# Three chunk buffers, a later gate product, smaller background steps and f16 selection in a two-block transformer kernel

## The chip, the cores and the metric

One core of one Trainium2 chip runs the whole program in one launch. The metric is the device time of one execution in microseconds (us). Engines are named as in the profile: PE (matmul), PEld (its weight loads), DVE (vector), ACT (scalar, which also issues DMAs), POOL (GpSimd, which issues the indirect DMAs), SP (which issues most DMAs).

## The reference, cut to what matters

Two blocks follow each other. The first has two layers; in each, a mixer (attention, pooling, a short convolution) is followed by a mixture of single experts. Layer 0 does this for 256 tokens and 256 context rows together, layer 1 for the 256 tokens. The experts are what the change is about:

```python
s1, i1 = lax.top_k(s[:, :, 0], 16)
s2, i2 = lax.top_k(s[:, :, 1], 16)
cand = (s1[..., :, None] + s2[..., None, :]).reshape(128, 8, 256)
cidx = (i1[..., :, None] * 128 + i2[..., None, :]).reshape(128, 8, 256)
top_s, pos = lax.top_k(cand, 16)
eidx = jnp.take_along_axis(cidx, pos, axis=-1)
gate = jax.nn.softmax(top_s, axis=-1)
hid = jax.nn.gelu(jnp.einsum('td,thkd->thk', xc, u_emb[eidx]))
return jnp.einsum('thk,thkd->td', gate * hid, v_emb[eidx])
```

Each row of 1024 values picks 8 times 16 of 16384 experts. An expert's number is 128 times a first index plus a second one, both below 128. The second block (feed-forward, retention, block attention, convolution) is not touched.

## The kernel before, in words

Every f32 matrix is multiplied as three products of halves: ACT rounds a 128 x 1024 weight tile `raw` to `wh` (`_high`, line 212), DVE or POOL subtracts to get the rest `wl` (`_low`, line 223), and PE multiplies high by high, high by low and low by high. `Stream` hands the tiles out in one fixed order (`plan`); its loads (`raw`, five buffers) are issued on SP as buffers come free. `pool_every = n` sends every n-th subtraction to POOL.

**The experts, dense part.** For three of layer 0's four tiles of 128 rows (384 columns, `TD`), and all of layer 1's, the kernel multiplies by all experts. In the *first expert stage* (loop over 128 tiles of `in_u`) PE computes x times u, ACT applies the gelu into `gstage` (line 1642) and stores two of them at a time to DRAM (`gel`, line 1647). Meanwhile the gates are worked out in the background and stored as a dense matrix (`gmat`, 128 experts by 32 rows at a time). In the *second expert stage* (loop over 128 tiles of `in_vv`) hidden values and gates come back in chunks: `wload` (lines 1595 and 1597, on SP) loads `gelc` and `gmc`, four steps' worth for layer 0 (`CI` = 4) and 768 KB each, `wmul` (line 1604, on DVE for layer 0) multiplies them in place, `wsplit` makes `Wh` (ACT, line 472) and `Wl` (DVE, line 473) for the step two ahead, and `vmm` (line 1692) does 18 matmuls of 512 columns a step. Two chunks have buffers: chunk c + 2 is loaded in the last step of chunk c, and chunk c + 1 multiplied in the first step of chunk c.

**The experts, gathered part.** Layer 0's fourth tile fetches the 128 rows of u and 128 rows of v that each of its rows needs by indirect DMAs (POOL, line 1399, four buffers of 128 x 1024), and DVE does one pass over each (line 1408 for u, 1423 for v). These 256 passes are spread: some in the first expert stage, some in the second, and the rest in the convolution part of layer 1's mixer (`tail`), where each of 35 units does its share. The modulation of layer 1 is made in the same second stage by DVE from tiles `in_modt` (line 516).

**The background.** In layer 0 `Side` decides where background pieces stand in the program: it counts a virtual time (`tick`, one step per few matmuls), books DVE and ACT time per piece (`took`, `use`), and lets a piece run when both engines' booked time lies at most `LIM` = 2000 ns ahead. A `yield step()` is a place where a weight tile's subtraction can come between two pieces. The pieces of `route`, for each tile of 128 rows: eight sums `cand` (line 1435), eight rounds of top 16, then for index and half a comparison `eq` (line 1463), its product with the index table `sif` (line 1465) and a sum (line 1466); then the gates, and from line 1556 the dense gate matrix.

```python
nc.vector.tensor_mul(eq, eq, sif[:, hh, i, None, :].to_broadcast([128, 4, 16, 16]))
```

In all of this the order on each engine is fixed when the program is built, and each engine runs its instructions in that order.

Of the kernel before, what the change touches and what calls it, by code (L numbers as in the profile page):

```python
# [10 lines left out]
F32 = mybir.dt.float32  # L11
# [249 lines left out]
LIM = 2000  # L261
# [8 lines left out]
class Side:  # L270
# [8 lines left out]
    def __init__(self, period, ring):  # L279
        self.lanes, self.lates = [], []  # L280
        self.period, self.ring = period, ring
        self.now = self.due = 0.0
        self.slot = [0.0] * 4
        self.free = {"a": 0.0, "v": 0.0, "p": 0.0}
        self.seq = 0
        self.floor = False
        self.rate, self.pe = RATE, 1.0

    def _advance(self, lane):
        try:  # L290
# [83 lines left out]
    def tick(self, dt):  # L374
        self.now += dt * self.pe
        while True:
            while any(x[0] <= self.now for x in self.lates):
                self._late()
            if self.now < self.due or max(self.free["v"], self.free["a"]) > self.now + LIM:
                return  # L380
            for lane in self.lanes:
                if self._ready(lane[1]) <= self.now:
                    self._run(lane)
                    break
            else:
                return
# [18 lines left out]
def tile_dit_peer_conformer(ctx: ExitStack, tc: tile.TileContext, A, out):  # L405
# [834 lines left out]
    def seg_tail(pool, ns, upd, halves, hs, ss, ab, banks, fill=None, then=None):  # L1240


        xs = two_rows(pool, upd, halves, hs[0:2], ss[0], 2 if fill is None else 4)

        def rest(*ts):
            for t in ts:
                for dh in halves:
                    upd(t, dh)

        if fill is None:  # L1250
            norm_cols(pool, xs, ab[0], 0, 2 if ns == 2 else 3, banks, then)
            W.pool_every = 0 if ns == 1 else 2
            W.pump(3)
            if ns == 2:
                rest(2)
            return
        rest(2)
        norm_cols(pool, xs, ab[0], 0, 3, banks, then)
        rest(3)
        xs = norm_rows(pool, hs[2:4], ss[1], 4)  # L1260
        for k in range(2):
            fill(k, 0)
        norm_cols(pool, xs, ab[1], 256)
        for k in range(2):
            fill(k, 1)
# [4 lines left out]
    def peer(l, hcp, kp, keys, early):  # L1270
# [14 lines left out]
        with ExitStack() as st:  # L1285
# [72 lines left out]
            TKW = 2.0  # L1358
            side = cur["side"] = W.side = Side(0.0 if sp else 24 * T / 2.4 / (nt + 1.3), ring)
            if sp:  # L1360
                side.rate, side.pe = RATE2, 1.09
            sel = select()
            side.add(sel)
            W.pool_every = 1
# [63 lines left out]
            def route():  # L1428
                for t in (range(nt) if not sp else (3, 0, 1, 2)):
                    v4 = sv[:, t].rearrange("p (h i) k -> p h i k", i=2)  # L1430
                    cand = tk.tile([128, 8, 16, 16], F32, name="cand", bufs=1)
                    if sp:
                        yield step()
                    for h in range(8):
                        (nc.vector if sp else nc.gpsimd).tensor_add(cand[:, h], v4[:, h, 0, :, None].to_broadcast([128, 16, 16]),
                                                                    v4[:, h, 1, None, :].to_broadcast([128, 16, 16]))
                    took("v", 3000)
                    ts = tk.tile([128, 8, 16], F32, name="ts", bufs=2)
                    pos = tk.tile([128, 8, 16], U32, name="pos", bufs=2)
                    yield step()  # L1440
# [11 lines left out]
                    nc.vector.tensor_scalar(ab[:, 1], pos, 15, None, op0=OP.bitwise_and)  # L1452
                    abf = tk.tile([128, 2, 8, 16], F32, name="abf", bufs=1 if sp else 2)
                    nc.vector.tensor_copy(abf, ab)
                    sif = tk.tile([128, 8, 2, 16], F32, name="sif", bufs=1 if sp else 2)
                    nc.vector.tensor_copy(sif, si[:, t].rearrange("p (h i) k -> p h i k", i=2))
                    took("v", 1100)
                    yield step()
                    for i in range(2):
                        for h0 in (0, 4):  # L1460
                            hh = slice(h0, h0 + 4)
                            eq = tk.tile([128, 4, 16, 16], F32, name="eq", bufs=1)
                            nc.vector.tensor_tensor(eq, abf[:, i, hh, :, None].to_broadcast([128, 4, 16, 16]),
                                                    iota16[:, None, None, :].to_broadcast([128, 4, 16, 16]), op=OP.is_equal)
                            nc.vector.tensor_mul(eq, eq, sif[:, hh, i, None, :].to_broadcast([128, 4, 16, 16]))
                            nc.vector.tensor_reduce(IN[:, t, i].rearrange("p (h k) -> p h k", h=8)[:, hh], eq, axis=AX.X, op=OP.add)
                            took("v", 3700)
                            yield step(TKW * 1.3)
                    nc.vector.tensor_sub(GN[t].rearrange("p (h k) -> p h k", h=8), ts, ts[:, :, 0:1].to_broadcast([128, 8, 16]))
                    if sp:  # L1470
# [84 lines left out]
                for q in range(0, TD // 4, 2):  # L1555
                    if sp:
                        yield paced(q)
                    Am = tg.tile([128, 8, 128], F16, name="Am", bufs=3)
                    Bk = tg.tile(shape, F16, name="Bk", bufs=2)
                    Bm = tg.tile([128, 2] + shape[1:], F16, name="Bm", bufs=3)  # L1560
                    nc.vector.tensor_tensor(Am, iotac[:, None, :].to_broadcast([128, 8, 128]),
                                            IT[:, 1, q * 4:q * 4 + 8, None].to_broadcast([128, 8, 128]), op=OP.is_equal)
                    nc.vector.tensor_tensor(Bk, iotas, spread(IT[:, 0], q), op=OP.is_equal)
                    took("v", 1950)
                    if len(pend) > 2:
                        flush(*pend.pop(0))
                    yield paced(q + 1)
                    for n in range(2):
                        nc.vector.tensor_mul(Bm[:, n], Bk, spread(GT[:, n], q))
                    done = took("v", 1420)  # L1570
                    if len(pend) > 2:
                        flush(*pend.pop(0))
                    pend.extend((q + j, Am[:, 4 * j:4 * j + 4], Bm[:, :, 2 * j:2 * j + 2], done) for j in range(2))
                    if not sp:
                        yield
# [15 lines left out]
            ld, ww = {}, {}  # L1591

            def wload(c):
                g = vq.tile([128, CI, TD], F32, name="gelc", bufs=2)
                nc.sync.dma_start(g, gel_d[c])
                m = vq.tile([128, ntb, CI, TB], F32, name="gmc", bufs=2)
                nc.sync.dma_start(m, g_d[:, :, c * CI:(c + 1) * CI, :].rearrange("b p c t -> p b c t"))
                ld[c] = (g, m)

# [11 lines left out]
            def wsplit(i):  # L1611
                c, r = divmod(i, CI)
                g = ld[c][0]
                wh = vp.tile([128, TD], F32R, name="Wh", bufs=4)
                wl = vp.tile([128, TD], F32R, name="Wl", bufs=4)
                split(wh, wl, g[:, r])
                if sp:
                    took("a", 470)
# [7 lines left out]
            for i in range(128):  # L1626
# [1 line left out]
                    wsplit(0)  # L1628
                    wsplit(1)
                if i % GB == 0:  # L1630
                    gs = gp.tile([128, GB, TD], F32, name="gstage", bufs=3)
                h, lo = W.next("u", l, i)
                half = i % per
                if half == 0:
# [17 lines left out]
                if i == 118:  # L1652
# [6 lines left out]
                    vp = st.enter_context(tc.tile_pool(name=f"pv{l}", bufs=2))  # L1659
                    vq_stack = ExitStack()  # L1660
                    vq = vq_stack.enter_context(tc.tile_pool(name=f"pw{l}", bufs=2))
                    wload(0)
                    wload(1)
                    if l == 0:
                        def turn():
                            for _ in angles(vq):
# [29 lines left out]

            for i in range(128):
                c, r = divmod(i, CI)
                if r == 0 and c + 1 < nch:
                    wmul(c + 1)  # L1700
                if i + 2 < 128:
                    wsplit(i + 2)
                if r == CI - 1 and c + 2 < nch:
                    wload(c + 2)
                hl = W.next("vv", l, i, 1 if i >= 126 else None)
                if i >= 126:
# [730 lines left out]
```

## Time and profile before

| what | us |
|---|---|
| median of 3 runs | 4544.48 (4543.31 to 4550.07) |
| the profiled execution's own time | 4539.79 |
| its span, first to last instruction | 4538.0 |
| PE busy | 4215.3 (93%) |
| DVE busy | 3221.3 (71%) |
| ACT busy | 1970.2 (43%) |
| POOL busy | 1128.6 (25%) |
| DMA moved | 932.29 MB, 205 GB/s over the span |

The profiled execution lies 4.7 us below the median of the runs. Busy PE is pipelined matmuls and not PE at its peak: the granted clock (1.00 is 2.4 GHz, 0.50 is 1.2 GHz) stands in the windows. Layer 0's first expert stage ends at about 1444 us, its second runs from there to about 2206 us, and the gathered rest ends at about 2372 us. Layer 1's second expert stage runs from 3144 to 3502 us.

### The profile page before, as it was taken

The page shows a single profiled execution, that of the slowest core. Times are in us where ns is not written, and L with a number is a line of the kernel's source. Part 1 is how long each engine was busy: PE and PEld are TensorE (multiplying, and loading weights), DVE is VectorE, ACT ScalarE, POOL GpSimd, SP SyncE. Part 2 cuts the span into 40 slices and gives each one's busy share as a digit, 9 for nine tenths or more (in the row PEclk, how much of TensorE's full clock was granted, in tenths as well). Part 3 has the DMA queues.
Part 4 walks back from the last instruction along what each step waited for, and adds up shares of the span by engine and source line. Part 5 has one row for each costly group of instructions (what it writes and reads, how often), then busy time and mean ns, then how long its engine had stood idle before and what let it go on. Part 6 is the DMA issues. An engine that isn't in the chain of part 4 may idle for free. (4 is left out here: it accounts for less than half of the span.)

```text
span 4538.0 us, 66430 instructions
## 1 busy us (share of the span) xinstructions
PE 4215.3 (93%) x25423; PEld 3735.4 (82%) x25423; DVE 3221.3 (71%) x5177; ACT 1970.2 (43%) x2939; POOL 1128.6 (25%) x871
## 2 busy tenths in 40 slices
PE   8999999999998877777779989999999999999999
PEld 5887878999997666666678879999887998999988
DVE  6747766999996766566786878786666577555855
ACT  4224443334662222222334444575445445444544
POOL 0012343333117412222543446201443000000000
PEclk9999999999999888888899989999999999999999
DMA  6532232456889877878783336778886644556344
GB/s 218 166 99 69 72 101 97 151 194 234 293 293 343 278 259 270 289 276 283 249 301 110 107 124 206 237 282 306 281 280 237 215 154 132 187 181 215 116 160 156
DMA packets 304824, 932.29 MB, mean 205 GB/s; under 512 B 27752, under 2 KB 95736, under 8 KB 299640
## 3 DMA queue, kind: packets, MB, share of 16 engines
q1 hardware_dynamic: 244000, 696.86, 46.1%
q0 software_dynamic: 37040, 135.29, 8.3%
q10 hardware_dynamic: 23464, 95.88, 5.6%
q8 instruction: 199, 3.26, 0.3%
q14 instruction: 121, 0.99, 0.1%
HBM read 841.94 MB, written 85.99 MB: 204 GB/s over the span
## 5 line engine op out<-in xcount | busy, mean ns | idle before, releaser
L212 ACT ACTIVATE wh<-raw 128x1024 fp32r<-128x1024 f32 (+1 forms) x1086 | 1131.4, 1045 | 1093.4 <-DMA raw<-in_vv 516.4
L469 PE MATMUL pA<-xH,wl 128*128 128x256 f32 (+2 forms) x4600 | 1422.0, 309 | 57.3 <-DVE wl L223 46.1
L223 DVE TENSOR_TENSOR wl<-raw,wh 128x1024 fp32r<-128x1024 f32 (+2 forms) x956 | 1185.5, 1249 | 365.2 <-issue 185.5
L467 PE MATMUL pA<-xH,wh 128*128 128x256 f32 (+2 forms) x4600 | 1439.6, 313 | 1.7 <-ACT xH L472 1.3
L468 PE MATMUL pA<-xL,wh 128*128 128x256 f32 (+2 forms) x4600 | 1417.2, 308 | 0.5 <-DVE xL L473 0.3
L469 PEld LDWEIGHTS pA<-xH,wl 128*128 128x128 f32 x4600 | 876.1, 190 | 93.0 <-DVE wl L223 55.4
L467 PEld LDWEIGHTS pA<-xH,wh 128*128 128x128 f32 x4600 | 877.0, 191 | 34.8 <-issue 6.0
L468 PEld LDWEIGHTS pA<-xL,wh 128*128 128x128 f32 x4600 | 877.1, 191 | 26.6 <-DVE xL L473 1.1
L223 POOL TENSOR_TENSOR wl<-raw,wh 128x1024 fp32r<-128x1024 f32 (+1 forms) x130 | 322.8, 2484 | 731.8 <-PE pA L469 362.8
L1692 PE MATMUL pA<-wl,Wh 128*128 128x512 f32 x1024 | 349.9, 424 | 150.4 <-DVE wl L223 150.4
L1692 PEld LDWEIGHTS pA<-wl,Wh 128*128 128x128 f32 x1024 | 203.2, 202 | 211.1 <-DVE wl L223 163.9
L1692 PE MATMUL pA<-wh,Wl 128*128 128x512 f32 x1024 | 344.5, 419 | 1.7 <-DVE Wl L473 1.7
L1692 PE MATMUL pA<-wh,Wh 128*128 128x512 f32 x1024 | 335.3, 409 | 6.2 <-ACT Wh L472 6.2
L1399 POOL DMA_INDIRECT gr<-in_ur,gi x128 | 185.8, 1451 | 530.9 <-DVE gr L1408 498.8
L468 PE MATMUL pA<-wl,xH 128*128 128x256 f32 (+2 forms) x800 | 272.1, 340 | 10.2 <-POOL wl L223 6.2
L467 PE MATMUL pA<-wh,xH 128*128 128x256 f32 (+2 forms) x800 | 277.9, 347 | 1.8 <-ACT xH L472 1.8
L469 PE MATMUL pA<-wh,xL 128*128 128x256 f32 (+2 forms) x800 | 271.5, 339 | 1.1 <-DVE xL L473 1.1
L1399 POOL DMA_INDIRECT gr<-in_vr,gi x128 | 176.3, 1377 | 340.1 <-DVE gx L1423 297.7
L1609 POOL TENSOR_TENSOR gelc<-gelc,gmc 128x256 f32<-128x256 f32 x128 | 147.9, 1189 | 422.4 <-DMA gmc<-gmat 398.6
L1692 PEld LDWEIGHTS pA<-wh,Wl 128*128 128x128 f32 x1024 | 206.8, 202 | 54.5 <-DVE Wl L473 2.4
L1692 PEld LDWEIGHTS pA<-wh,Wh 128*128 128x128 f32 x1024 | 200.3, 196 | 56.2 <-ACT Wh L472 6.5
L458 POOL TENSOR_TENSOR segr<-segr,nhalf 128x1 f32<-128x1 f32 (+1 forms) x24 | 13.9, 579 | 886.3 <-DVE segr L547 886.3
(456 smaller groups left out, 6305.4 us busy)
## 6 DMA issues: line engine op xcount, KB each, us to landing
raw<-in_u SPq DMA_DIRECT2D x256, 512.0 KB
raw<-in_vv SPq DMA_DIRECT2D x256, 512.0 KB
raw<-in_modt SPq DMA_DIRECT2D x80, 512.0 KB
gmat<-gst ACTq DMA_DIRECT2D x20, 2048.0 KB
raw<-in_conv SPq DMA_DIRECT2D x48, 512.0 KB
raw<-in_gate SPq DMA_DIRECT2D x48, 512.0 KB
gel<-gstage ACTq DMA_DIRECT2D x64, 384.0 KB
gelc<-gel SPq DMA_DIRECT2D x32, 768.0 KB
```

The source lines that it names most:

```text
L212: self.nc.scalar.activation(h[:, :w], t[:, :w], AF.Copy)
L223: e.tensor_sub(lo[:, :w], t[:, :w], h[:, :w].bitcast(F32))
L458: nc.gpsimd.tensor_tensor(r, r, nhalf[:, 0:1].to_broadcast([128, w]), op=OP.pow)
L467: nc.tensor.matmul(o, s[0], m[0], start=start, stop=False)
L468: nc.tensor.matmul(o, s[0], m[1], start=False, stop=False)
L469: nc.tensor.matmul(o, s[1], m[0], start=False, stop=stop)
L1399: nc.gpsimd.indirect_dma_start(t, None, tabs[j // 128], bass.IndirectOffsetOnAxis(ap=gi[:, k:k + 1], axis=0))
L1609: nc.gpsimd.tensor_mul(gv, gv, m[:, :, ci])
L1692: nc.tensor.matmul(acc[t][dh], s_, m_[:, dh * 512:(dh + 1) * 512], start=(i == 0 and n == 0), stop=(i == 127 and n == 2))
```

## The change

Layer 0 (`sp`) alone gets three buffers each for `gelc` and `gmc`: three chunks are loaded before its second expert stage, then chunk c + 3 in the third step of chunk c, and chunk c + 1 is multiplied in the third step of chunk c. In exchange `Wh` and `Wl` go from four buffers to three, and `gstage` from three to two. `Side` gets its own limit for DVE, 1200 ns in layer 0, and the steps of `route` are cut smaller. `eq` and `sif` become f16 in both layers. `pool_every` is 0 and no longer 2 after layer 0's experts.

```diff
@@ -286,3 +286,3 @@
         self.floor = False
-        self.rate, self.pe = RATE, 1.0
+        self.rate, self.pe, self.lim = RATE, 1.0, LIM
 
@@ -378,3 +378,3 @@
                 self._late()
-            if self.now < self.due or max(self.free["v"], self.free["a"]) > self.now + LIM:
+            if self.now < self.due or self.free["v"] > self.now + self.lim or self.free["a"] > self.now + LIM:
                 return
@@ -1251,3 +1251,3 @@
             norm_cols(pool, xs, ab[0], 0, 2 if ns == 2 else 3, banks, then)
-            W.pool_every = 0 if ns == 1 else 2
+            W.pool_every = 0
             W.pump(3)
@@ -1360,3 +1360,3 @@
             if sp:
-                side.rate, side.pe = RATE2, 1.09
+                side.rate, side.pe, side.lim = RATE2, 1.09, 1200
             sel = select()
@@ -1434,5 +1434,7 @@
                     for h in range(8):
+                        if sp and h == 4:
+                            yield step()
                         (nc.vector if sp else nc.gpsimd).tensor_add(cand[:, h], v4[:, h, 0, :, None].to_broadcast([128, 16, 16]),
                                                                     v4[:, h, 1, None, :].to_broadcast([128, 16, 16]))
-                    took("v", 3000)
+                        took("v", 380)
                     ts = tk.tile([128, 8, 16], F32, name="ts", bufs=2)
@@ -1454,3 +1456,3 @@
                     nc.vector.tensor_copy(abf, ab)
-                    sif = tk.tile([128, 8, 2, 16], F32, name="sif", bufs=1 if sp else 2)
+                    sif = tk.tile([128, 8, 2, 16], F16, name="sif", bufs=1 if sp else 2)
                     nc.vector.tensor_copy(sif, si[:, t].rearrange("p (h i) k -> p h i k", i=2))
@@ -1461,8 +1463,14 @@
                             hh = slice(h0, h0 + 4)
-                            eq = tk.tile([128, 4, 16, 16], F32, name="eq", bufs=1)
+                            eq = tk.tile([128, 4, 16, 16], F16, name="eq", bufs=1)
                             nc.vector.tensor_tensor(eq, abf[:, i, hh, :, None].to_broadcast([128, 4, 16, 16]),
                                                     iota16[:, None, None, :].to_broadcast([128, 4, 16, 16]), op=OP.is_equal)
+                            took("v", 1250)
+                            if sp:
+                                yield step()
                             nc.vector.tensor_mul(eq, eq, sif[:, hh, i, None, :].to_broadcast([128, 4, 16, 16]))
+                            took("v", 1250)
+                            if sp:
+                                yield step()
                             nc.vector.tensor_reduce(IN[:, t, i].rearrange("p (h k) -> p h k", h=8)[:, hh], eq, axis=AX.X, op=OP.add)
-                            took("v", 3700)
+                            took("v", 1250)
                             yield step(TKW * 1.3)
@@ -1562,4 +1570,5 @@
                                             IT[:, 1, q * 4:q * 4 + 8, None].to_broadcast([128, 8, 128]), op=OP.is_equal)
+                    took("v", 1250)
                     nc.vector.tensor_tensor(Bk, iotas, spread(IT[:, 0], q), op=OP.is_equal)
-                    took("v", 1950)
+                    took("v", 700)
                     if len(pend) > 2:
@@ -1593,5 +1602,5 @@
             def wload(c):
-                g = vq.tile([128, CI, TD], F32, name="gelc", bufs=2)
+                g = vq.tile([128, CI, TD], F32, name="gelc", bufs=3 if sp else 2)
                 nc.sync.dma_start(g, gel_d[c])
-                m = vq.tile([128, ntb, CI, TB], F32, name="gmc", bufs=2)
+                m = vq.tile([128, ntb, CI, TB], F32, name="gmc", bufs=3 if sp else 2)
                 nc.sync.dma_start(m, g_d[:, :, c * CI:(c + 1) * CI, :].rearrange("b p c t -> p b c t"))
@@ -1613,4 +1622,4 @@
                 g = ld[c][0]
-                wh = vp.tile([128, TD], F32R, name="Wh", bufs=4)
-                wl = vp.tile([128, TD], F32R, name="Wl", bufs=4)
+                wh = vp.tile([128, TD], F32R, name="Wh", bufs=3 if sp else 4)
+                wl = vp.tile([128, TD], F32R, name="Wl", bufs=3 if sp else 4)
                 split(wh, wl, g[:, r])
@@ -1630,3 +1639,3 @@
                 if i % GB == 0:
-                    gs = gp.tile([128, GB, TD], F32, name="gstage", bufs=3)
+                    gs = gp.tile([128, GB, TD], F32, name="gstage", bufs=2 if sp else 3)
                 h, lo = W.next("u", l, i)
@@ -1661,4 +1670,4 @@
                     vq = vq_stack.enter_context(tc.tile_pool(name=f"pw{l}", bufs=2))
-                    wload(0)
-                    wload(1)
+                    for c in range(3 if sp else 2):
+                        wload(c)
                     if l == 0:
@@ -1698,3 +1707,3 @@
                 c, r = divmod(i, CI)
-                if r == 0 and c + 1 < nch:
+                if r == (CI - 2 if sp else 0) and c + 1 < nch:
                     wmul(c + 1)
@@ -1702,3 +1711,5 @@
                     wsplit(i + 2)
-                if r == CI - 1 and c + 2 < nch:
+                if sp and r == CI - 2 and c + 3 < nch:
+                    wload(c + 3)
+                if not sp and r == CI - 1 and c + 2 < nch:
                     wload(c + 2)
```

Second expert stage of layer 0, SP's queue, the loads of two chunks among the weight tiles (`vv`) and modulation tiles (`modt`); before:

```order
L1595 DMA gelc<-gel_7_5865 128x1536
L1597 DMA gmc<-gmat_5890 128x12x128
L200 DMA raw<-in_vv 128x1024
L200 DMA raw<-in_modt 128x1024
L200 DMA raw<-in_vv 128x1024 x3
L1595 DMA gelc<-gel_8_5866 128x1536
```

and in the changed program:

```order
L1604 DMA gelc<-gel_8_5866 128x1536
L1606 DMA gmc<-gmat_5890 128x12x128
L200 DMA raw<-in_modt 128x1024
L200 DMA raw<-in_vv 128x1024 x2
L200 DMA raw<-in_modt 128x1024
L200 DMA raw<-in_vv 128x1024 x2
L1604 DMA gelc<-gel_9_5867 128x1536
```

The loads keep their distance of four weight tiles, but stand one chunk further ahead of their use. DVE in the same stage, from one gate product on; before (names with their numbers, which tell the chunks apart):

```order
L1604 TENSOR_TENSOR gelc_13922<-gelc_13922,gmc_13924 128x1536 [waits DMAHW7_49,DMAHW0_49]
L473 TENSOR_TENSOR Wl_13957<-gelc_13792,Wh_13956 128x384 [waits PE_49,Activation_49]
L223 TENSOR_TENSOR wl_13964<-raw_13859,wh_13926 128x1024 [waits DMAHW4_49,PE_49]
L473 TENSOR_TENSOR Wl_13987<-gelc_13792,Wh_13986 128x384 [waits PE_49,Activation_49]
L223 TENSOR_TENSOR wl_13992<-raw_13898,wh_13962 128x1024 [waits DMAHW6_49,PE_49]
L1408 SCALAR_TENSOR_TENSOR gr_13784,gz_5918<-gr_13784,gx_5917 128x1024 [waits DMASW4_49]
L473 TENSOR_TENSOR Wl_14018<-gelc_13922,Wh_14017 128x384 [waits PE_49,Activation_49]
```

and in the changed program:

```order
L1613 TENSOR_TENSOR gelc_13722<-gelc_13722,gmc_13724 128x1536 [waits DMAHW1_49,DMAHW0_49]
L473 TENSOR_TENSOR Wl_13992<-gelc_13722,Wh_13991 128x384 [waits PE_49,Activation_49]
L223 TENSOR_TENSOR wl_14001<-raw_13904,wh_13963 128x1024 [waits DMAHW3_49]
L1408 SCALAR_TENSOR_TENSOR gr_13847,gz_5918<-gr_13847,gx_5917 128x1024 [waits DMASW3_49]
```

The product now stands directly ahead of the first split that needs it; before, two splits of the chunk in hand came between. DVE in layer 0's `route`, around the second tile's candidate sums; before:

```order
L1484 TENSOR_TENSOR gn<-gn,smx 128x128
L1435 TENSOR_TENSOR cand<-sv 128x256 x8
L1443 MAX ts<-cand 128x8
L1444 MAX_INDEX pos<-ts,cand 128x8
L1445 MATCH_REPLACE cand<-ts,cand 128x256
L1446 MAX ts<-cand 128x8
L1447 MAX_INDEX pos<-ts,cand 128x8
L223 TENSOR_TENSOR wl<-raw,wh 128x1024
```

and in the changed program, at the third tile:

```order
L1492 TENSOR_TENSOR gn_5913<-gn_5913,smx 128x128
L1437 TENSOR_TENSOR cand<-sv 128x256 x4
L223 TENSOR_TENSOR wl<-raw,wh 128x1024
L1437 TENSOR_TENSOR cand<-sv 128x256 x4
L1445 MAX ts<-cand 128x8
```

Eight sums in a row became four and four with a weight tile's subtraction between them. Over the whole program the passes over gathered rows (lines 1408 and 1423) that stand ahead of the first gate product are 55 and were 65; inside the second expert stage they are 131 and were 134; behind it, in layer 1's convolution part, they are 69 and were 56. The five subtractions that POOL had in that last part are DVE's.

## Rows read from the trace of the kernel before

**Rows 1.** The page of the kernel before
```profile
span 4538.0 us, 66430 instructions
```

**Rows 2.** Busy time of each engine by stage, with granted clock and DMA
```profile
core 0: us, PE busy (x) PEld busy (x) DVE busy (x) ACT busy (x) POOL busy (x), PEclk, DMA share, GB/s
852.00:1390.00 538.00, 523.42 (x3439) 504.80 (x3438) 498.98 (x774) 279.75 (x331) 142.92 (x78) 0.99 0.71 252
1390.00:1444.00 54.00, 38.20 (x202) 36.24 (x200) 31.23 (x45) 14.35 (x23) 41.69 (x53) 0.92 0.96 352
1444.00:2206.00 762.00, 605.50 (x2292) 473.78 (x2292) 504.06 (x628) 193.97 (x269) 233.32 (x192) 0.87 0.80 278
2206.00:2372.00 166.00, 128.90 (x893) 122.36 (x894) 142.35 (x159) 51.97 (x77) 89.66 (x68) 0.88 0.78 276
...
2690.00:3144.00 454.00, 450.49 (x4040) 446.13 (x4041) 356.48 (x657) 269.72 (x318) 134.82 (x75) 1.00 0.72 249
3144.00:3502.00 358.00, 358.00 (x1536) 287.56 (x1536) 234.31 (x260) 174.66 (x257) 133.37 (x112) 1.00 0.79 273
```

**Rows 3.** Waits, 1444 to 2206 us: who for whom: us in total, times, longest
```profile
ACT wh L212 <- DMA raw<-in_vv: 515.3, 102, 10.8
...
DVE gelc L1604 <- DMA gmc<-gmat: 243.9, 29, 10.4
...
PE pA L1692 <- DVE wl L223: 150.4, 31, 7.8
```

**Rows 4.** Busy times inside one chunk of four steps of that stage
```profile
1716.00:1728.00 12.00, 12.00 (x53) 9.63 (x52) 5.01 (x8) 2.94 (x4) 2.62 (x2) 1.00 1.02 355
...
1730.00:1732.00 2.00, 0.00 (x0) 0.00 (x0) 1.98 (x2) 0.00 (x0) 0.00 (x0) 0.95 0.24 94
...
1734.00:1736.00 2.00, 2.00 (x6) 1.58 (x5) 2.00 (x4) 0.00 (x0) 0.00 (x0) 0.50 0.78 223
```

**Rows 5.** DVE's groups, 1444 to 2206 us: busy us, mean ns of one, idle before
```profile
L1604 DVE TENSOR_TENSOR gelc<-gelc,gmc 128x1536 f32<-128x1536 f32 x31 | 54.6, 1763 | 243.9 <-DMA gmc<-gmat 243.9
```

**Rows 6.** Busy times at the end of that stage
```profile
2180.00:2200.00 20.00, 20.00 (x83) 16.04 (x82) 19.73 (x22) 6.54 (x8) 10.25 (x8) 0.94 0.94 346
```

**Rows 7.** Busy times inside the stretch that follows it
```profile
2310.00:2330.00 20.00, 16.06 (x124) 15.45 (x123) 19.16 (x23) 3.59 (x5) 11.01 (x9) 0.95 0.90 327
```

**Rows 8.** Busy times of ten us at the first expert stage's end
```profile
1400.00:1410.00 10.00, 8.40 (x39) 8.36 (x40) 3.72 (x6) 3.06 (x7) 7.56 (x12) 0.66 1.06 391
```

**Rows 9.** Waits of PE, 852 to 1390 us
```profile
PE pA L469 <- DVE wl L223: 12.8, 6, 3.0
PE pA L469 <- POOL wl L223: 1.7, 2, 1.4
```

**Rows 10.** DVE in order of time around one tile's candidate sums
```profile
956.03 7.97 DVE L1435 TENSOR_TENSOR cand<-sv 128x256 f32<-128x256 f32 x8
...
966.31 1.21 DVE L223 TENSOR_TENSOR wl<-raw,wh 128x1024 fp32r<-128x1024 f32 x1
```

**Rows 11.** ACT's stores of hidden values, both layers; the last of layer 0
```profile
L1647 ACTq DMA_DIRECT2D gel<-gstage x96: 325/326/1590, 818.6 to 3144.8; - x96
...
1445.84 0.33 ACTq L1647 DMA_DIRECT2D gel<-gstage  x1
```

**Rows 12.** DVE's groups, 852 to 1444 us, shapes apart
```profile
L1569 DVE TENSOR_TENSOR Bm<-Bk,GT 128x1024 f16<-128x1024 f16 x96 | 61.9, 686 | 0.9
...
L1465 DVE TENSOR_TENSOR eq<-eq,sif 128x1024 f32<-128x1024 f32 x16 | 28.0, 1748 | 0.5
```

**Rows 13.** Groups on DVE and POOL, then PE's waits, 2206 to 2372 us
```profile
L1423 DVE SCALAR_TENSOR_TENSOR gx<-gr,gz,gx 128x1024 f32<-128x1024 f32 x55 | 74.8, 1360 | 12.8 <-DMA gr<-in_vr,gi 12.0
...
L223 POOL TENSOR_TENSOR wl<-raw,wh 128x1024 fp32r<-128x1024 f32 x5 | 12.7, 2530 | 9.7 <-ACT wh L212 9.6
...
PE pA L469 <- DVE wl L223: 23.6, 17, 5.3
...
PE pA L469 <- POOL wl L223: 9.2, 3, 3.9
```

## Prediction

> **What bounds the kernel now.** I read the page first: a span of 4538.0 us [rows 1]. Then the busy times by stage, looking for stages in which PE is not the limit. Layer 1's second expert stage shows what PE alone needs: it is busy all of 358.00 us for 1536 matmuls of 512 columns at a granted clock of 1.00, so 0.233 us each [rows 2]. Layer 0's second expert stage does 128 steps of 18, which at that pace is 2304 x 0.233 = 537 us; it takes 762.00, at a mean clock of 0.87 [rows 2]. So 225 us there are not matmul work at full clock, and this is the stage to look at. DVE is busy for 504.06 of the 762 us and DMA runs at a share of 0.80, 278 GB/s: each has room on average [rows 2].
>
> The waits of the stage say who is late. PE stood 150.4 us for DVE's subtraction `wl`; DVE stood 243.9 us, 29 times, for the loads of the gates `gmc`; ACT stood 515.3 us for weight tiles [rows 3]. The first two are one event seen from two engines, and the windows inside one chunk show it. From 1716 to 1728 the DMA engines are full (share 1.02, 355 GB/s) and PE runs at 1.00; then DVE, which has stood behind its product since before 1728, starts again. In 1730 to 1732 PE does nothing, and the DMA has fallen to 94 GB/s, because the weight buffers are full and only DVE's work frees them; in 1734 to 1736 PE works again, but at 0.50, the 1.2 GHz level [rows 4]. A chunk thus pays for the wait three times: PE idles, PE restarts slowly, and the DMA loses time that it must make up. The wait stands directly ahead of the product, whose own work is small: 31 of 1763 ns against 243.9 us of idle time [rows 5].
>
> **The change, part by part.** *Third buffers and the later product (layer 0's second expert stage).* A chunk is now loaded eight steps ahead of its product instead of about one. At 18 x 0.233 = 4.2 us a step that is some 33 us, against waits that were at most 10.4 us long [rows 3]. So I take this wait as gone. On SP the load of chunk c + 3 waits for the last split of chunk c, one step earlier; the weight tiles queued behind it wait for subtractions of that same step, so it holds up none of them. What is late next is not PE but the DMA. The stage moved 762 us x 278 GB/s = 211.8 MB [rows 2]. The order shows three gathered passes less in it (0.52 MB each), and one chunk of 1.57 MB is loaded ahead of it, so 208.7 MB remain. The rate at which it can move them while PE and DVE are both busy comes from two rows. Near the end of the stage, with PE busy 20.00 of 20 us and DVE 19.73, it was 346 GB/s [rows 6]; behind the stage, with DVE at 19.16 of 20, it was 327 [rows 7]. I take the middle, 336: 208.7 MB / 336 GB/s = 621 us. PE fits into that even if its clock stayed at 0.87 throughout (537 / 0.87 = 617), and so does DVE with its 504. **762 to 621 is -141 us.** The ends: at the 355 GB/s of the best long window [rows 4] it is 588 us, -174; the poor end is the first rival below.
>
> For the whole-stage rate there is also a rule. Ten us near the end of the first expert stage ran at 391 GB/s [rows 8], so nothing in the trace stops the DMA at 355. The Trainium skill (DMA: Bandwidth & Descriptors, Specifications) gives an HBM limit of about 358 GB/s a core; by it the stage would take an estimated 583 us and the sum below would be -167 instead of -129. The ten us lie above it, and the measurement decides.
>
> *The product next to its first split.* Before, two splits stood between; now `Wh` and `Wl` of the next chunk follow at once. PE is two steps or 8.4 us behind, and the product takes 1.76 [rows 5]: I cost it at 0. If that cover were gone, it would cost up to 1.76 us per chunk, 56 us in all, but then the DMA bound above hides it too.
>
> *`Wh` and `Wl` with three buffers.* `Wl` now waits for the PE step that `wl`, which has three buffers already, waits for right behind it in DVE's queue: 0. Behind `Wl` on DVE stand `wl`, the gathered passes and the modulation, and PE waits for `wl`; they have the same two steps of slack.
>
> *The third chunk ahead of the stage.* 1.57 MB more stand on SP ahead of the last two `u` tiles and the first `vv` tiles, in a stretch where the DMA is full (share 0.96, 352 GB/s, PE busy 38.20 of 54.00 [rows 2]): 1.57 / 352 = 4.5, so **+4 us**.
>
> *Smaller steps and the limit of 1200 ns (first expert stage).* PE waited 12.8 + 1.7 us there [rows 9], and a mean clock of 0.99 over 538.00 us [rows 2] costs another 5.4: at most 20 us can come back. Eight candidate sums stood in a row for 7.97 us, and with one round of the top 16 behind them DVE brought no subtraction from 956.03 to 966.31 [rows 10], while PE uses up two tiles (DVE's and POOL's) in 9.8 us; this pace is that of the 64 stores, one for two tiles, from 818.6 to 1445.8 [rows 11]. Now four sums come between two subtractions, but the order puts three rounds (2.3 us each, from the 2.4 us behind the sums [rows 10]) behind the second four, 4.0 + 6.9 = 10.9 us. Some of the stalls will stay: I take half, **-10 us**, ends 0 and -20.
>
> *f16 selection.* With f16 on both sides, 1024 products take 686 ns where today's take 1748 [rows 12]: 16 x 1.06 = 17 us of DVE in layer 0, and in layer 1 half as many. The work that hides them is PE's own, busy 523.42 of 538.00 and 450.49 of 454.00 us [rows 2], and layer 0's stalls are counted above: 0. The comparison and the sum keep an f32 side and are left at their price.
>
> *The gathered rest and `pool_every` (1444 to 2372 us).* The smaller limit lets ten passes less into the first expert stage; with the three from the second, 13 more come into layer 1's convolution part. There DVE is busy 142.35 of 166.00 us and DMA runs at 276 GB/s [rows 2], so nothing hides them: 13 x 1.36 us [rows 13] = 17.7 of DVE, or 13 x 0.52 MB / 276 = 25 of DMA. Five subtractions come over from POOL [rows 13], at 1.21 each [rows 10]: 6. DVE's 24 at its present share of 86% are 28 us; PE's wait for POOL, 9.2 us [rows 13], goes. **+18 us**, ends +8 and +30.
>
> **The sum**: -141 + 4 - 10 + 18 = -129. Against the profiled execution's 4539.79 that is 4411; the median of the runs lies 4.7 us higher, so I predict **4415 us**.
>
> **The rivals.** *Forecast*, 60%: the second stage comes down to 590 to 655 us, bound by DMA.
>
> *A: the DMA does not keep up,* 22%. Weight tiles, chunks and gathered rows come in bursts from two queues, and the stretch behind the stage, which has no gate product at all, reached only 276 GB/s with PE waiting 23.6 us for `wl` [rows 2, 13]. Half way between 276 and 346 [rows 6], 311 GB/s, gives 671 us: -91 instead of -141, so 4465. Against it: that stretch has a start-up with little DMA in it.
>
> *B: PE becomes the bound,* 8%. The stage falls to 537 us, -225, the sum to -213: 4331. It needs 208.7 / 537 = 389 GB/s throughout; ten us ran at 391 [rows 8], but the twelve of a full chunk at 355 [rows 4].
>
> *C: two stage buffers hold ACT up,* 5%, and the kernel is slower. A store leaves every 9.8 us [rows 11]. With three buffers it has 9.8 x 2 + 4.9 = 24.5 us to land before the gelu of a later tile needs its buffer, with two 14.7. ACT shows no wait on it today, so it lands within 24.5. If it took that long, a pair of tiles would take (24.5 + 4.9) / 2 = 14.7 us instead of 9.8; over the 32 pairs in the later half, where the gates' stores of 2048 KB share the queue, this is +157, and with the -129 the time is 4572. It decides from a landing of 14.7 us, and outweighs the gain from about 22.7 us (4.0 a pair over 32 pairs). ACT then also delays the `wh` for which PE waits.
>
> *D: the change does not do what it says,* 5%. The wait for `gmc` goes, but ACT's wait for weight tiles, 515.3 us and longer than it [rows 3], fills the same time: the stage stays at 762, and 4 - 10 + 18 = +12 gives 4556. Against it: the DMA stands nearly still while DVE waits [rows 4], so ACT's wait is itself partly made by it.
>
> **How the numbers follow.** About 0.2%, 9 us, is what a measurement of this kernel can tell from no change. Forecast, A and B are faster: 90%. C and D leave 10%; D lies near the limit, so 3% for no change and 7% for slower. Low end: -174 - 20 + 4 + 8 = -182, 4362. High end: A with its poor ends, -91 + 0 + 4 + 30 = -57, 4487, and a little for a rate below 311. 4360 to 4492 leaves out B, C and D, 18%.
>
> **What would show it.** In the changed profile DVE's wait for `gmc` should be near 0 and the second stage about 620 us with a DMA share of 0.93 or more and a clock above 0.9; the first expert stage's PE waits about 7 us; `eq` times `sif` near 0.7 us; the convolution part about 185 us with DVE waiting for nothing long. I am wrong if the second stage stays over 700 us, if ACT waits for its stores, or if PE's wait for `wl` there stays near 150 us.

## The result, and the profile after

The changed kernel takes 4354.5 us (median of 4 runs, 4353.94 to 4358.45) against 4543.9 for the kernel before on the same chip (4533.0 to 4550.07): a ratio of 0.9588, 95% interval 0.9568 to 0.9607, so 189 us less. Forecast were 4415 us with a range of 4360 to 4492. The profiled execution took 4358.45 us. Its page:

```profile
span 4356.6 us, 66320 instructions
...
PE 4167.9 (96%) x25423; PEld 3704.6 (85%) x25423; DVE 3201.0 (73%) x5180; ACT 1968.1 (45%) x2939; POOL 1121.0 (26%) x868
```

Busy time by stage, with columns and stages as in [rows 2]; the bounds are moved to where these stages now lie:

```profile
core 0: us, PE busy (x) PEld busy (x) DVE busy (x) ACT busy (x) POOL busy (x), PEclk, DMA share, GB/s
852.00:1376.00 524.00, 518.24 (x3428) 501.23 (x3427) 481.64 (x798) 279.01 (x332) 127.21 (x70) 0.99 0.70 248
1376.00:1430.00 54.00, 43.90 (x216) 41.77 (x216) 31.98 (x45) 14.05 (x22) 39.16 (x51) 0.87 1.02 375
1430.00:2003.00 573.00, 549.85 (x2295) 432.77 (x2293) 498.30 (x630) 191.46 (x265) 246.62 (x191) 0.99 1.00 364
2003.00:2192.00 189.00, 136.84 (x911) 130.73 (x910) 160.97 (x183) 53.11 (x81) 91.40 (x77) 0.85 0.80 285
...
2507.00:2959.00 452.00, 449.06 (x4041) 445.09 (x4041) 346.52 (x658) 270.58 (x319) 132.74 (x75) 1.00 0.73 250
2959.00:3317.00 358.00, 358.00 (x1536) 287.56 (x1535) 235.96 (x259) 174.70 (x257) 131.50 (x112) 1.00 0.79 273
```

The second expert stage of layer 0 (third line of times) is where the time went: 573.00 us instead of 762.00, clock 0.99 instead of 0.87, DMA share 1.00 instead of 0.80. PE is busy for 549.85 of it. DVE worked as long as before, 498.30 us. Layer 1's two stages in the last lines moved by at most 2 us.

Who waited for whom in that stage, as in [rows 3]:

```profile
ACT wh L212 <- DMA raw<-in_vv: 238.8, 67, 8.2
...
ACT Wh L472 <- DVE gelc L1613: 110.2, 28, 13.1
...
PE pA L1701 <- DVE wl L223: 16.2, 17, 3.9
```

DVE's wait for `gmc`, 243.9 us before, has no row any more. PE's wait for `wl` is 16.2 us where it was 150.4. ACT now stands 110.2 us behind the product that comes directly ahead of its split; PE's own wait for that split `Wh` is 5.9 us.

To compare runs, four marks are taken from each trace: the first gelu of layer 0, its first `vmm` matmul, the first transpose behind the second expert stage, and the last gathered pass. In us between the marks:

| kernel | first stage | second stage | gathered rest | to the end |
|---|---|---|---|---|
| before | 631.1 | 762.2 | 166.8 | 2164.9 |
| changed | 618.1 | 575.9 | 184.8 | 2165.6 |

The differences, -13.0, -186.3, +18.0 and +0.7, make -180.6; the spans differ by 4356.6 - 4538.0 = -181.4. The medians differ by 8 us more, less than the 17 us over which the runs of before spread. The marks come from one execution of each kernel. How far they vary by themselves shows where the program is the same: the first stage of before took 631.1 us and, in a run below with the same first stage, 627.8; the second stage of the changed kernel took 575.9, 573.1 and 571.7 in three runs that do not touch it; the last column goes from 2161.5 to 2172.9 among the variants of the changed kernel. A difference of five us between two stages is therefore not shown by them.

### The profile page after: what moved, and what is told of

Its sections match the earlier page's. It is cut to its first block, busy times and chain, and to the rows that moved or that the text cites. A ratio compares the mean times of both kernels' runs of the same rounds, so it can differ in the third digit from the quotient of the medians.

```text
span 4356.6 us, 66320 instructions
## 1 busy us (share of the span) xinstructions
PE 4167.9 (96%) x25423; PEld 3704.6 (85%) x25423; DVE 3201.0 (73%) x5180; ACT 1968.1 (45%) x2939; POOL 1121.0 (26%) x868
## 5 line engine op out<-in xcount | busy, mean ns | idle before, releaser
L223 DVE TENSOR_TENSOR wl<-raw,wh 128x1024 fp32r<-128x1024 f32 (+1 forms) x959 | 1173.1, 1232 | 372.5 <-issue 181.7
L223 POOL TENSOR_TENSOR wl<-raw,wh 128x1024 fp32r<-128x1024 f32 (+1 forms) x127 | 312.5, 2460 | 718.3 <-PE pA L469 326.7
L1701 PE MATMUL pA<-wl,Wh 128*128 128x512 f32 x1024 | 328.1, 401 | 16.3 <-DVE wl L223 16.2
L1701 PE MATMUL pA<-wh,Wh 128*128 128x512 f32 x1024 | 325.3, 398 | 5.9 <-ACT Wh L472 5.9
L1701 PE MATMUL pA<-wh,Wl 128*128 128x512 f32 x1024 | 325.2, 398 | 1.0 <-DVE Wl L473 1.0
L1701 PEld LDWEIGHTS pA<-wl,Wh 128*128 128x128 f32 x1024 | 191.9, 189 | 71.2 <-DVE wl L223 25.9
L1399 POOL DMA_INDIRECT gr<-in_vr,gi x128 | 186.0, 1453 | 216.7 <-DVE gx L1423 171.4
L473 DVE TENSOR_TENSOR Wl<-gelc,Wh 128x384 fp32r<-128x384 f32 (+1 forms) x256 | 137.6, 538 | 139.2 <-ACT Wh L472 138.1
```

Source lines behind the costliest of these rows:

```text
L223: e.tensor_sub(lo[:, :w], t[:, :w], h[:, :w].bitcast(F32))
L473: nc.vector.tensor_sub(lo, src, h.bitcast(F32))
L1399: nc.gpsimd.indirect_dma_start(t, None, tabs[j // 128], bass.IndirectOffsetOnAxis(ap=gi[:, k:k + 1], axis=0))
L1701: nc.tensor.matmul(acc[t][dh], s_, m_[:, dh * 512:(dh + 1) * 512], start=(i == 0 and n == 0), stop=(i == 127 and n == 2))
```

## The experiments

All ratios are to the kernel before, run beside each series on the same chip; the changed kernel has 0.9588. It was not run again beside the series, so a kernel is compared with it by these ratios. "Stages" are the four columns of the table. The forecast gave the gain to two things at once, third buffers and a later product, and put smaller steps beside them. The first four runs take these apart.

**The chunk part alone.** Into the kernel before go the hunks of `wload`, `wmul`, `Wh`, `Wl` and `gstage`, and nothing else.

> The kernel before with the chunk part alone: three buffers, the late product, three Wh/Wl, two gstage. Theory 1 (the wait for the gates in layer 0's second expert stage is the whole gain): the stage falls from 762 to about 575 us as in the changed kernel, and since the gathered passes keep their old places the convolution part stays at 166: 4544 - 187 + 4 = 4361 us (4350 to 4372). Theory 2 (smaller steps, the limit and f16 bring a good part, because DVE is freed ahead of the stage): the stage stays over 620 us, the time over 4400.

4357.56 us, ratio 0.9601 (0.9577 to 0.9624). Stages: 631.8, 580.4, 165.2, 2163.9. Theory 1 holds: 4361 us were expected, and the second stage lies 5 us above the 575 of the theory.

**Everything but the chunk part.** The same hunks undone in the changed kernel.

> The changed kernel with the chunk part undone. Theory 1: the stage is back at about 760 us with a wait for the gates near 240 us; the first expert stage keeps its gain of some 14 us and the convolution part its loss of 20, so 4544 + 6 = 4550 us (4535 to 4565). Theory 2: under 4500.

4534.26 us, ratio 0.9994 (0.9983 to 1.0006): no difference from the kernel before, and 1 us below the range of theory 1. Stages: 614.8, 747.8, 188.1, 2161.5. In these marks the smaller steps and what goes with them win 16 us in the first stage and 14 in the second, and lose 21 behind it. But the traced execution, at 4523.32 us, was the fastest of ten, and the 14 us, with a wait for the gates of 180.4 instead of the expected 240, were not foreseen; their cause is not shown. The waits of the second stage are back (1447 to 2005 us):

```profile
DVE gelc L1613 <- DMA gmc<-gmat: 180.4, 23, 10.4
...
PE pA L1701 <- DVE wl L223: 117.6, 24, 10.8
```

**The late product with two buffers**, one line of the kernel before:

```diff
-                if r == 0 and c + 1 < nch:
+                if r == (CI - 2 if sp else 0) and c + 1 < nch:
```

> The kernel before with the product moved to the third step and nothing else; two buffers. A chunk then has three steps, 12.6 us at full pace, between load and product instead of one. Theory 1a (distance in time is all that matters, and a load of 1.57 MB behind weight tiles lands in about 13 us): most of the wait goes, stage 590 to 660 us, 4375 to 4445 us. Theory 1b (the third buffer is needed, since the wait only moves to the split that needs the product at once): stage over 700 us, over 4485 us.

4358.5 us, ratio 0.9598 (0.9573 to 0.9622). Stages: 627.8, 588.4, 167.1, 2167.5. Better than theory 1a had it: one line brings 174 of the 186 us of the second stage. Its waits from 1450 to 2000 us:

```profile
PE pA L1692 <- DVE wl L223: 14.8, 16, 1.2
...
DVE gelc L1604 <- DMA gmc<-gmat: 6.0, 6, 2.0
```

DVE still meets the load at times, but 6 times for 6.0 us in all. A distance of three steps is enough without a third buffer.

**Three buffers with the early product.** As the first run, but with `r == 0` kept.

> As the first run of this series, but the product stays in the first step of a chunk; six steps, 25 us, between load and product. Theory 1a: no wait for the gates either, same time as with the late product, within 8 us (about 4361). Theory 1b (the late product matters by itself, because DVE then has less in front of the weight tiles): slower than it by over 20 us.

4360.45 us, ratio 0.9612 (0.9589 to 0.9635). Stages: 631.0, 588.1, 165.4, 2162.6. The wait for the gates has no row here either. So either half alone, loading earlier or multiplying later, gives nearly all. Both together give 8 us more by the marks (588 against 580 in the second stage), which the whole times, 4357.56 against 4358.5 and 4360.45, can't confirm.

**What bounds the stage now.** In `wload` of the changed kernel, for layer 0:

```diff
-                m = vq.tile([128, ntb, CI, TB], F32, name="gmc", bufs=3 if sp else 2)
+                if sp and c:
+                    ld[c] = (g, ld[0][1])
+                    return
+                m = vq.tile([128, ntb, CI, TB], F32, name="gmc0" if sp else "gmc", bufs=1 if sp else 2)
```

> The changed kernel, but in layer 0 the gates of chunk 0 are loaded once and used for all chunks (31 loads of 786 KB left out, 24 MB of some 209 in the second expert stage; the experts' output is another). Theory 5 (after the change that stage is bound by DMA, share 1.00): it falls from 576 us to PE's own 545 to 550, and 4 us more go ahead of it: about 4325 us. Theory 6 (PE with its waits is the bound and the DMA only fills up because it may): stage 570 or more, 4345 us or over.

4326.94 us, ratio 0.9532 (0.9514 to 0.955). Stages: 618.1, 551.6, 185.9, 2161.6. Theory 5: with 24 MB less to load the stage falls by 24 us, close to PE's own time. At 364 GB/s 24 MB are 66 us; they are not all won, because PE then bounds the stage. The 4 us ahead of the stage did not come: the first stage is 618.1 as before. The busy times (columns as above) and waits of 1450 to 1960 us:

```profile
1450.00:1960.00 510.00, 505.26 (x2153) 405.16 (x2153) 468.03 (x591) 185.60 (x247) 222.19 (x167) 0.99 0.94 342
```

```profile
ACT wh L212 <- DMA raw<-in_vv: 80.4, 50, 6.0
...
PE pA L1704 <- DVE wl L223: 4.7, 2, 3.8
```

PE is busy 505.26 of 510 us, the DMA share has fallen below 1, and PE's wait for `wl` is 4.7 us where it was 16.2 in the whole stage. In the changed kernel the DMA is the bound, PE close behind.

**f32 selection.** `eq` and `sif` back to `F32` in the changed kernel.

> The changed kernel with eq and sif in f32 again. Forecast's theory (the f16 product is hidden behind PE): same time within 6 us, the product near 1.24 us in the middle instead of 0.69. Rival (DVE is full in the first expert stage and every us of it counts): first expert stage longer by 8 to 17 us.

4361.09 us, ratio 0.9609 (0.959 to 0.9628). Its interval overlaps that of the changed kernel. But the first stage took 627.7 us, and the three kernels with the first stage of the changed one (the changed kernel itself, the run above and the `pool_every` run below) took 618.1 each time. So the stages speak for the rival, 9.6 us, though the whole time doesn't settle it. PE's waits of 852 to 1376 us in the f32 run, which the account of the prediction comes back to:

```profile
PE pB L1514 <- DVE gn L1492: 4.8, 1, 4.8
PE pA L469 <- POOL wl L223: 3.6, 2, 2.0
PE pA L469 <- DVE wl L223: 3.5, 3, 1.9
```

The product's own duration (ns, least, median and most, both layers), f32 first and then the changed kernel:

```profile
L1470 DVE TENSOR_TENSOR eq<-eq,sif x24: 1224/1225/3349, 892.7 to 2711.2; 128x1024 f32<-128x1024 f32 x24
```

```profile
L1470 DVE TENSOR_TENSOR eq<-eq,sif x24: 691/692/2861, 893.1 to 2702.7; 128x1024 f16<-128x1024 f16 x24
```

**DVE's limit.** `side.lim` at 2000, and then at 2600, in the changed kernel.

> The changed kernel with DVE's limit back at 2000 ns; smaller steps stay. By the order, gathered passes are 65 ahead of, 129 inside and 61 behind the second expert stage (changed kernel: 57, 128, 70 by the same count). Theory 3 (the limit alone pushed passes into the convolution part, at about 1.5 us a pass, and the smaller steps alone removed PE's stalls): convolution part 185 - 13 = 172 us, first expert stage unchanged within 3 us, 4354 - 13 = 4341 us. Theory 4 (the limit is what keeps DVE's queue short, so the stalls return): first expert stage up by 10 us or more, no gain in all.

These counts cut the order at other places than those in the section on the change, which has 55, 131 and 69 for the changed kernel.

4350.99 us, ratio 0.9589 (0.9573 to 0.9606). Stages: 623.6, 582.2, 168.3, 2172.9. No gain, as theory 4 has it, though for another reason: the rest got its 16 us back as in theory 3, the first and second stage gave up 5.5 and 6.3, and the part to the end, whose program is the same, took 7.3 longer in this execution.

> The changed kernel with the limit at 2600 ns: passes 72, 130 and 53. Theory 3: convolution part about 160 us, 4354 - 25 = 4329 us. Theory 4: the first expert stage gives back 15 us or more, 4345 us or over.

4332.57 us, ratio 0.9545 (0.9529 to 0.9562): faster than the changed kernel, the intervals of the ratios don't meet. Stages: 615.2, 585.2, 149.7, 2168.8. Theory 3 holds, and the rest is even shorter than its 160 us. 17 passes fewer take 35 us from the rest, 2.1 us each. 15 of them went ahead of the second stage, where the first stage did not suffer, and two into it. The second stage is 9 us longer, more than two passes of 0.52 MB at 364 GB/s would cost; why, and why the first stage was longer at 2000, stays open.

> The changed kernel with the limit at 4000 ns: passes 74, 132 and 49. If only the place of the passes counts: 4 fewer behind the second stage than with 2600, 5 us faster than that. If the length of DVE's queue counts (theory 4): the first expert stage loses 10 us or more against 2600.

4327.76 us, ratio 0.9531 (0.9515 to 0.9547). Stages: 621.7, 585.9, 143.4, 2166.9. The rest wins 6 us on 2600, the first stage loses 6.5, less than the 10 of theory 4: in time the two are the same.

**Limit 2600 and a pass booked at 1200 ns**, `took("v", 1200)` instead of 1310:

> The limit of 2600 ns, and a gathered pass booked at 1200 ns instead of 1310: passes 77, 136 and 42 (with 2600 alone 72, 130, 53). If a pass behind the second stage costs 2 us, as in the run with 2600 (35 us for 17), one inside it 0.52 MB at 364 GB/s or 1.4 us, and one ahead of it little: convolution part 150 - 22 = 128, second stage +8, so some 12 us faster than with 2600 alone. Rival (DVE's queue now gets too long for the weight tiles): the second and first stage take it back, 0 or slower.

4321.33 us, ratio 0.9505 (0.9487 to 0.9524). Stages: 619.3, 594.5, 131.7, 2166.5. The fastest kernel of the series, 0.9% below the changed one (0.9505 / 0.9588). Against limit 2600 alone, 11 passes fewer took 18 us from the rest, 1.6 each. Six more in the second stage came with 9 us there and five more ahead of it with 4 in the first stage, so the marks, of the slowest of five executions, show 5 us of gain, where the ratios differ by 0.4%. That it is the difference of the prices of a pass in two places is an argument from these sums.

**Limit 2600 with two buffers** (four `Wh`, `Wl`, three `gstage`, the late product kept):

> The changed kernel at 2600 ns with two chunk buffers, four Wh/Wl, three gstage, and the late product kept. Theory 1a (the distance that the late product gives is nearly enough): second stage 8 to 12 us longer than with three buffers, 4333 + 8 = 4341 us by the series before. Rival (third buffer matters more when more passes compete for the DMA): 20 us or more.

4334.58 us, ratio 0.9542 (0.9525 to 0.9559). Stages: 615.9, 589.9, 152.1, 2164.4. The second stage is 4.7 us longer than with three buffers, less than the 8 to 12 expected, and within what such marks vary by: here no worth of the third buffer is shown.

**pool_every at 2.** `W.pool_every = 0 if ns == 1 else 2` again.

> The changed kernel with pool_every at 2 again behind layer 0's experts: some subtractions of layer 1's convolution part go back to POOL. Forecast's term (five subtractions cost DVE 6 us there, PE's waits for POOL of 9 us go): the convolution part within 5 us of 185, no difference in time beyond 6 us. Rival (DVE is the bound there, so every subtraction taken off it counts with its waits): 8 us or more faster.

4359.53 us, ratio 0.9596 (0.958 to 0.9612). Stages: 618.1, 571.7, 190.4, 2165.1. No difference in time, as the forecast's term has it; the convolution part is 5.6 us longer than in the changed kernel, where at most 5 were expected. PE's waits from 2003 to 2195 us, which answer to those of the kernel before in [rows 13]:

```profile
PE pA L469 <- DVE wl L223: 37.2, 18, 4.9
PE pA L469 <- POOL wl L223: 10.0, 4, 4.0
```

POOL takes subtractions off DVE, but PE then waits for POOL: 47.2 us in all, where it waited 44.3 for DVE alone in the changed kernel.

## Why the prediction was wrong

**What bounds, and the wait: right.** The stage, the wait and its three prices (idle PE, 1.2 GHz after it, an idling DMA) were named, and taking the wait away gave them back: clock 0.99, share 1.00.

**The step that failed is the rate at which the DMA can move 208.7 MB: 336 GB/s, and so 621 us and -141.** Of the 60 us between the forecast's -129 and the measured -189, 45 lie in this term (-141 against -186), 7 in the first stage, and 8 in how far the traced execution lies from the median. The bytes were right: 573.00 us x 364 GB/s are 208.6 MB. The rate was 364. The forecast took it from windows in which PE and DVE were both busy, as if these were then at the DMA's limit, at 346 and 327 GB/s [rows 6, 7]. Their shares were 0.94 and 0.90: the DMA was not full in them, and the rate was what the others asked of it. At a full share they stand for 346 / 0.94 = 368 and 327 / 0.90 = 363, and 208.7 MB at 365 is 572 us, 4 from the measured 575.9. That this comes so near is in part luck: the same division of the whole stage before, 278 / 0.80 [rows 2], gives 348 and 600 us. The range's low end, 355 from one chunk [rows 4], was read at a full share, but over 12 us only, and the rate at a full share is no constant. Three of the changed kernel's windows of 30 us in the second stage:

```profile
1520.00:1550.00 30.00, 28.77 (x122) 22.53 (x121) 27.49 (x39) 9.15 (x13) 7.23 (x5) 1.00 1.00 354
...
1670.00:1700.00 30.00, 29.31 (x126) 23.28 (x125) 25.36 (x35) 10.37 (x15) 8.56 (x7) 1.00 1.03 395
...
1880.00:1910.00 30.00, 29.00 (x117) 22.93 (x118) 26.97 (x31) 9.95 (x14) 10.78 (x7) 0.94 1.05 389
```

They run from 354 to 395 GB/s at shares of 1.00 to 1.05. The rate depends on what is moved, as the packets in the trace show. Over the stage (1430 to 2003 us) the gates came in packets of 512 bytes, 22.8 MB at 17.4 GB/s per busy DMA engine; the weight and modulation tiles came in packets of 4096 bytes, 91.7 MB at 24.0. The gates are thus 11% of the bytes and 14% of the DMA engines' time. This does not order the three windows, which hold about 1.5, 1.6 and 1.0 MB of gates, so what else moves the rate stays open.

The prediction cites from the Trainium skill (DMA: Bandwidth & Descriptors, Specifications) an HBM limit of about 358 GB/s a core. The stage moved more than that, 364 over its whole length. But the estimate by that limit, 583 us, lies 7 us from the measured 575.9, and the forecast's 621 lies 45 from it. The prediction had read 391 GB/s over ten us [rows 8] and still let its range end at 355.

**Rival B** (PE becomes the bound, 537 us) was given 8%. It was wrong in name, since the run with the gates loaded once shows that the DMA is, but its time was as near as the forecast's: the stage ended 39 us from B's and 45 from the forecast's. The two bounds lay closer together than the forecast saw: 576 us as bound by DMA, and 552 with the gates loaded once, where PE bounds. **Rival A** was the same error again: a stage with a share of 0.78 is no measure of what the DMA can do.

**The distance in time.** The forecast compared eight steps, 33 us, with waits of at most 10.4 us, and did not ask what less would do. Three steps do nearly as well.

**The third chunk ahead (+4), the smaller steps (-10) and f16 (0)** make -6; measured -13.0, and made of other parts. The third chunk's +4 is not settled: with the old steps the first stage took 631.8 and 631.0 us with it and 631.1 and 627.8 without, with the new ones 618.1 and 614.8. Of PE's waits in the first stage (852 to 1376 us) these are left, with [rows 9] as 12.8 and 1.7 before:

```profile
PE pB L1514 <- DVE gn L1492: 4.0, 1, 4.0
PE pA L469 <- DVE wl L223: 1.4, 2, 1.0
PE pA L469 <- POOL wl L223: 0.3, 1, 0.3
```

They are 5.7 us in all, where 14.5 stood before and 7 were forecast. But the f32 run has the same small steps, and its three waits above make 11.9: the steps took DVE's `wl` from 12.8 to 3.5, and waits for `gn` and for POOL came in its place. So the smaller steps and the limit by themselves bring 2.6 us of waits in this window and 3.4 of the stage (631.1 to 627.7, about what such marks vary by). f16, costed at nothing behind PE, brings 6.2 us of waits in the window and 9.6 of the stage. That the two terms' sum is near the measured one is luck. The price of f16 was wrong too: 1748 ns was a mean that held four slow products of sixteen, and the f16 mean is 1222 and not 686 (last section). That frees 16 x 0.526 = 8.4 us of DVE and not 17. That this is no longer hidden because DVE, too, is near full in that stage (481.64 of 524.00) is an argument.

**The gathered rest (+18)**: measured +18.0; that it is so exact is luck, since the same moves without the chunk part gave +21.3. DVE's groups and PE's wait there, as in [rows 13]:

```profile
L1423 DVE SCALAR_TENSOR_TENSOR gx<-gr,gz,gx 128x1024 f32<-128x1024 f32 x69 | 90.5, 1312 | 18.1 <-DMA gr<-in_vr,gi 17.2
L223 DVE TENSOR_TENSOR wl<-raw,wh 128x1024 fp32r<-128x1024 f32 x36 | 43.9, 1221 | 0.0
```

```profile
PE pA L469 <- DVE wl L223: 44.3, 17, 5.7
```

14 passes more, as traced, and five subtractions more, with PE's wait for `wl` at 44.3 us instead of 23.6. `pool_every` by itself makes no difference in time; the number of passes does, as the runs with other limits show.

**Rival C** didn't come: ACT's gelu, which fills the stage buffers, waits for PE's products, and for no store (852 to 1430 us):

```profile
ACT gstage L1651 <- PE pA L469: 151.8, 62, 6.4
...
ACT gstage L1651 <- issue: 2.8, 1, 2.8
...
ACT gstage L1651 <- ACT gst L1540: 2.5, 6, 0.5
```

**Rival D** was wrong: ACT's wait for weight tiles fell from 515.3 to 238.8 us with the gates', so much of it was made by it.

## What to carry to other kernels

A transfer rate read from a trace is a limit only where the DMA share is 1; elsewhere it is what the engines asked for. Divided by the share it is a better estimate of the bound, here 348 to 368 GB/s by row against 364 measured, and packets of 512 bytes move less than those of 4096 in the same time. An in-order engine that waits for a load holds up everything that frees buffers, so the wait costs the DMA its time too; moving the use a few steps later can be worth as much as another buffer and costs no memory. When one stage becomes bound by a resource, background work should be priced by stage, and moved from where it costs most: here 1.6 to 2.1 us a pass behind the experts, no price that shows for the 15 that the limit of 2600 ns moved ahead of the second stage, and one inside that stage that the runs do not settle. Work that frees an engine can pay although another engine is the busier one; only a run that undoes it tells.

## What was not expected of the hardware

A DMA can be kept full for a whole stage: 364 GB/s at a share of 1.00 over 573 us, with weight tiles, chunks and gathered rows mixed.

The f16 product halves, from 1225 ns in the middle to 692, but its mean in the first expert stage was 1222:

```profile
L1470 DVE TENSOR_TENSOR eq<-eq,sif 128x1024 f16<-128x1024 f16 x16 | 19.5, 1222 | 0.5
```

Some take four times as long. DVE and then POOL around one of them, in order of time (start, us):

```profile
996.08 0.69 DVE L1470 TENSOR_TENSOR eq<-eq,sif 128x1024 f16<-128x1024 f16 x1
...
999.33 2.82 DVE L1470 TENSOR_TENSOR eq<-eq,sif 128x1024 f16<-128x1024 f16 x1
```

```profile
999.19 2.41 POOL L223 TENSOR_TENSOR wl<-raw,wh 128x1024 fp32r<-128x1024 f32 x1 [6.15 <-PE pA L469]
```

The one at 999.33 began 0.14 us after a subtraction on POOL and takes 2.82 us instead of 0.69. All sixteen such products of the first stage in all fourteen traces, 224, say the same. The 46 that began while a subtraction on POOL was under way took at least 2.78 us in f16 and 3.31 in f32. The other 178 took 0.68 to 0.69 and 1.22 to 1.23, and among these are 27 beside which POOL's subtraction began later. So what counts is which of the two begins first. No run took POOL's work away there, so the gain from moving it is not measured.
